# A hybrid retention, gating and convolution layer on one core: a ninth couple in the up product, two weight sums made by adding transfers, and three steps placed elsewhere

## The chip, the cores and the metric

The kernel runs on one core of a Trainium2 chip. The metric is the device time of one execution in microseconds (us); lower is better. A run here is one execution, and the times before are those of three runs.

## The reference

One layer of an encoder over 512 positions of width 1024, in float32:

```python
h = rmsnorm(x, g_pre_mix);  q, k, v, g, u, sv, a_ret, a_sgu = split(h @ w_in)
y_ret = (layernorm(retention(rotary(q), rotary(k), v)) * silu(g)) @ w_ret_o      # both directions, 4 heads
y_sgu = (gelu(u) * (w_spatial @ layernorm(gelu(sv)) + b_spatial)) @ w_sgu_o      # 128-position chunks
x = x + rmsnorm((sigmoid(a_ret) * y_ret + sigmoid(a_sgu) * y_sgu) @ w_out, g_post_mix)
h2 = rmsnorm(x, g_pre_ffn)
hid = depthwise_conv3(h2 @ w_up) + conv_b            # w_up is 1024 x 5632
a, b = split(hid, 2)
y = x + rmsnorm((gelu(a) * b) @ w_down, g_post_ffn)  # w_down is 2816 x 1024
```

## The kernel before, in words

All weights lie in one tensor `wall` of 146 blocks of 128 x 1024 (512 KB). A block or half block is loaded into a `raw` buffer (four of them) by a transfer that SP issues. It is then split into two float32r parts, so that three matmuls give nearly float32 precision: `split` (L112 to L114) has ACT round the value into the high part (L97) and DVE subtract that from the value into the low part (L114). The parts lie in nine `w4` buffers; `w_get` prepares weights up to eight half blocks ahead of their use, and a buffer comes free when PE has used it.

Where a product is big enough, four blocks of it are made by seven products of half size in place of eight (a Strassen-like scheme, `Pair`). `Pair.part1` makes four products, `part2` one, `part3` two, each of 12 matmuls of 256 columns (L915). A plain block (`f_block`) is 24 matmuls of 512 columns (L289 to L291). For a pair, `w_form` loads two blocks (B11, B12, B22, B21) and makes four sums of half blocks: T1 = B12 + B11 (L196), T3 = B12 + B22 in the place of B12 (L197), T2 = T1 + B22 (L199) and T4 = T2 + B21 in the place of T2 (L202). In the up product all four are DVE additions of 128 x 512.

The stages on which the change bears, in order of time:

- **The u blocks** (from 200 to 246 us). Four plain blocks, then pairs. Beside them the layer norm of `sv` is made: `sv_stats` (statistics of one row tile, DVE), `sv_scale` (POOL makes reciprocal roots and shifts from the statistics of all four tiles), `sv_norm(q)` (ACT scales four tiles of half q). These stand where `tc.issue_after(i)` puts them: behind instruction i.
- **The up product** (472 to 672 us). There are 22 tiles i, of two blocks each (a and b). Tiles 4 to 19 are done as eight couples, one after the other: a couple (i, i+1) does the blocks of tile i as a `Pair` and those of tile i+1 as two plain blocks; tiles 20 and 21 are plain. `tile_done` makes the convolution (`conv`, L1226 to L1233), the gate (`gated`), and at given tiles `down_forms`: the sums and splits of activations that the down product needs. Their low parts `fl` are made by an adding transfer that POOL issues (L1252).
- **The down product** (672 to 771 us), in two passes (columns 0 to 511, then 512 to 1023). Each of nine steps j takes weights "q" (768 wide) and their sums "t" (1024 wide, made by DVE at L217, L221 and L222), split into `dh` and `dl`, and does seven products (L1351). Steps of whole tiles stand between (L1367). Beside the steps 2 to 5 of pass two, `first_share` squares pass one's result and multiplies it by gffn (L1421, DVE).

No planner is written in the kernel. The framework orders each engine's instructions when the program is built, within the order of data and the `issue_after` marks; from then on every engine works through its list in order.

Of the kernel before, what the change touches and what calls it, by code (L numbers as in the profile page):

```python
# [13 lines left out]
ALU = mybir.AluOpType  # L14
# [3 lines left out]
S = 512  # L18
NT = S // P
# [8 lines left out]
SV0, U0, GATE0, GATE1 = 24, 32, 40, 72  # L28
# [9 lines left out]
UP0 = DOWN0 - 2 * NF  # L38
EARLY = 4
QK = (4, 0, 5, 1, 6, 2, 7, 3)  # L40
COUPLES = [(i, i + 1) for i in range(4, 20, 2)]

PRE, FFNG, LNG, LNB = 0, 8, 16, 24
CW, CB = 32, 32 + 3 * 2 * NF
# [5 lines left out]
def tile_block(ctx: ExitStack, tc, xT, x, wall, par, cs, wsp, bsp, gpost, gffn, out):  # L50
    nc = tc.nc
# [57 lines left out]
    def as32(t):  # L109
        return t.bitcast(F32)  # L110

    def split(hi, lo, src):  # L112
        copy(hi, src)
        nc.vector.tensor_sub(lo, src, as32(hi))  # L114

# [4 lines left out]
    i = 0  # L122
    while i < NW:
        pair = [(f, i) for f in FORMS]
        if i == SV0:
# [3 lines left out]
            i = U0  # L129
# [3 lines left out]
        elif GATE0 <= i < GATE1:  # L133
            units += pair[:4] + [("blk", i + 2)] + pair[4:] + [("blk", i + 3)]
            i += 4
        elif i == UP0 + 2 * COUPLES[0][0]:
            for a, b in COUPLES:
                pair = [(f, UP0 + 2 * a) for f in FORMS]
                units += pair[:4] + [("blk", UP0 + 2 * b)] + pair[4:] + [("blk", UP0 + 2 * b + 1)]
            i = UP0 + 2 * COUPLES[-1][1] + 2  # L140
        elif i == DOWN0:
# [9 lines left out]
    v = nc.vector  # L151
    w_ready, w_pos, w_held, w_raw = {}, [0, 0], [0], {}
# [32 lines left out]
    def w_form(form, i):  # L185

        if form == "B11":
            a, b = raw_tile(), raw_tile()
            nc.sync.dma_start(a, wall[i])
            nc.sync.dma_start(b, wall[i + 1])  # L190
            w_raw["B11"], w_raw["B12"] = a[:, :S], a[:, S:]
            w_raw["B22"], w_raw["B21"] = b[:, :S], b[:, S:]
        elif form == "T1":
            t = raw_tile()
            w_raw["T1"], w_raw["T2"], w_raw["T3"], w_raw["T4"] = t[:, :S], t[:, S:], w_raw["B12"], t[:, S:]
            nc.vector.tensor_add(w_raw["T1"], w_raw["B11"], w_raw["B12"])  # L196
            nc.vector.tensor_add(w_raw["T3"], w_raw["B12"], w_raw["B22"])  # L197
            eng = nc.vector if i < GATE0 or i >= UP0 else nc.gpsimd
            eng.tensor_tensor(out=w_raw["T2"], in0=w_raw["T1"], in1=w_raw["B22"], op=ALU.add)  # L199
        elif form == "T4":  # L200
            eng = nc.vector if i < GATE0 or i >= UP0 else nc.gpsimd
            eng.tensor_tensor(out=w_raw["T4"], in0=w_raw["T2"], in1=w_raw["B21"], op=ALU.add)  # L202
        w = slot("wf", 0, 1088)
        lo, hi = w[:, AT_64 : AT_64 + S], w[:, S + AT_192 : 2 * S + AT_192]
        split(hi, lo, w_raw[form])
        return hi, lo

    def w_down(form, i):
# [584 lines left out]
    def sv_stats(ts):  # L793
        for t in ts:
            for nh in range(2):
                v.bn_stats(out=sst[:, t, nh, :], in_=svz[t, nh])
            v.bn_aggr(out=smv[:, t, :], in_=sst[:, t].rearrange("p a b -> p (a b)"))
# [3 lines left out]
        rsqrt(srstd, smv[:, :, 1], 1.0, NT)  # L801
        shift(sshift, srstd)

    def sv_norm(q):
        for t in range(NT):
            scaled_to(svz[t, q], srstd[:, t : t + 1], sshift[:, t : t + 1])


# [164 lines left out]
    for j in range(UW):  # L973
        with tc.issue_after(summed) if j == 0 else ExitStack():
            o = f_block(xh, xl, KD)
        u = U_HOMES.pop()()
        i = v.tensor_mul(two(u), in_turn(o), two(rbc)).ins
        g = nc.scalar.activation(out=u, in_=u, func=AF.Gelu_apprx_tanh).ins
        uT.append(u)
        with tc.issue_after(i):  # L980
            sv_stats(((0, 1), (2,), (3,), ())[j])
        if j == 2:
            sv_scale()
    with tc.issue_after(g):
        sv_norm(0)
    for j in range(UW // 2, KD // 2):
        p = Pair(AF.Gelu_apprx_tanh, lambda: U_HOMES.pop()(), None, rbc)
        p.part1()
        if late:
            late.part3()  # L990
        p.part2()
        late = p
        uT += p.t
        if j == UW // 2:
            with tc.issue_after(p.copied):
                sv_norm(1)
    yh, yl = [], []

    def mix(j):
# [288 lines left out]
    def tile_done(i, o):  # L1288
        gated(*(conv(t, 2 * i + s_) for s_, t in enumerate(o)))
        if i < COUPLES[-1][1]:  # L1290
            if i in (7, 9, 11, 13, 17):
                down_forms(len(dforms))
        elif len(dforms) < EAGER:
            down_forms(len(dforms))
# [13 lines left out]

    couples = dict(COUPLES)
    i = 0  # L1310
# [100 lines left out]
    gpf = []  # L1411
    qn = [small("q", 4, 4) for _ in range(NT)]
    zg = []

    def first_share(t):
        zg.append(blk(n="zg"))
        for i in range(2):
            src = c4[2 * (t // 2) + i][:, (t % 2) * 256 : (t % 2 + 1) * 256]
            j = tmp("junk")
            nc.scalar.activation(out=j[:, :256], in_=src, func=AF.Square, scale=D ** -0.5, accum_out=qn[t][:, 2 + i : 3 + i])  # L1420
            v.tensor_mul(zg[t][:, i * 256 : (i + 1) * 256], src, gpf[0][:, i * 256 : (i + 1) * 256])  # L1421
        v.tensor_add(qn[t][:, 0:1], qn[t][:, 2:3], qn[t][:, 3:4])


# [140 lines left out]
def _up(a):  # L1565

    for i, _ in COUPLES:
        b, c = a[2 * i].reshape(P, 2, S), a[2 * i + 1].reshape(P, 2, S)
# [88 lines left out]
```

## Time and profile before

| | |
|---|---|
| three runs, median (lowest to highest) | 786.4 us (786.27 to 786.45) |
| the profiled execution, its own time | 787.56 us |
| its span, first to last instruction | 785.8 us |
| busy: PE, DVE, ACT, POOL | 99%, 80%, 59%, 13% of the span |
| granted TensorE clock | 0.997 |

The profiled execution is 1.16 us slower than the median of the runs, and its own time is 1.76 us longer than its span. In the timeline each matmul stands with its start, and with an end that is modelled: a matmul of 256 columns is shown as 0.28 us long although the next one starts 0.11 us later. So PE counts as busy through a pause that is shorter than this tail, and what PE loses is read from the distance of two starts.

### The profile page before, as it was taken

The page shows a single profiled execution, that of the slowest core. Times are in us where ns is not written, and L with a number is a line of the kernel's source. Part 1 is how long each engine was busy: PE and PEld are TensorE (multiplying, and loading weights), DVE is VectorE, ACT ScalarE, POOL GpSimd, SP SyncE. Part 2 cuts the span into 40 slices and gives each one's busy share as a digit, 9 for nine tenths or more (in the row PEclk, how much of TensorE's full clock was granted, in tenths as well). Part 3 has the DMA queues.
Part 4 walks back from the last instruction along what each step waited for, and adds up shares of the span by engine and source line. Part 5 has one row for each costly group of instructions (what it writes and reads, how often), then busy time and mean ns, then how long its engine had stood idle before and what let it go on. Part 6 is the DMA issues. An engine that isn't in the chain of part 4 may idle for free.

```text
span 785.8 us, 13253 instructions
## 1 busy us (share of the span) xinstructions
PE 777.3 (99%) x5067; PEld 720.5 (92%) x5067; DVE 626.2 (80%) x1067; ACT 467.2 (59%) x848; POOL 104.4 (13%) x132
## 2 busy tenths in 40 slices
PE   9999999999999999999999999999999999999996
PEld 8888998998899999999998898999999998999996
DVE  6467987788777877867765679989999889877887
ACT  6555558689375534444444776657777578744442
POOL 0040001130011111032210210001111012200001
PEclk9999999999999999999999999999999999999998
DMA  8782224463223333223349111435555365633244
GB/s 285 268 260 90 81 81 161 108 133 128 75 82 108 108 108 108 98 92 108 134 166 330 68 68 40 122 108 141 141 148 148 108 195 115 170 114 111 103 163 161
DMA packets 35888, 104.78 MB, mean 133 GB/s; under 512 B 4400, under 2 KB 6320, under 8 KB 35824
## 3 DMA queue, kind: packets, MB, share of 16 engines
q1 hardware_dynamic: 27936, 87.81, 32.6%
q0 software_dynamic: 7024, 14.95, 9.0%
q10 hardware_dynamic: 864, 1.18, 0.4%
q8 instruction: 39, 0.64, 0.3%
q14 instruction: 25, 0.20, 0.1%
HBM read 91.34 MB, written 4.19 MB: 122 GB/s over the span
## 4 chain that ended last, share of the span: by engine, by line
PE 96%; DVE 1%; ACT 1%; issue 1%; POOLq 0%; POOL 0%; DVEq 0%; ACTq 0%
PE ps L915 21%; PE ps L289 13%; PE ps L291 13%; PE ps L290 13%; PE ps L1351 10%; PE ps L744 5%; PE ps L623 4%; PE ps L625 4%; PE ps L624 4%; PE ps L1088 2%; PE ps L1086 2%; PE ps L1087 2%; PE ps L1367 2%; PE ps L1008 1%; PE ps L409 1%
## 5 line engine op out<-in xcount | busy, mean ns | idle before, releaser
L114 DVE TENSOR_TENSOR wl<-raw,wh 128x1024 fp32r<-128x1024 f32 (+1 forms) x88 | 100.6, 1152 | 55.6 <-issue 19.1
L97 ACT ACTIVATE wf<-raw 128x512 fp32r<-128x512 f32 x126 | 75.6, 623 | 85.8 <-PE ps L290 39.8
L97 ACT ACTIVATE wh<-raw 128x1024 fp32r<-128x1024 f32 (+2 forms) x92 | 89.2, 982 | 29.1 <-DMA raw<-wall 16.8
L915 PE MATMUL ps<-sh,wf 128*128 128x256 f32 x576 | 105.8, 276 | 0.5 <-ACT u L97 0.3
L114 DVE TENSOR_TENSOR wf<-raw,wf 128x512 fp32r<-128x512 f32 x126 | 92.3, 745 | 15.2 <-ACT wf L97 14.3
L915 PEld LDWEIGHTS ps<-sh,wf 128*128 128x128 f32 x576 | 91.8, 192 | 1.7 <-ACT u L97 1.1
L289 PE MATMUL ps<-h2h,wh 128*128 128x512 f32 (+1 forms) x256 | 90.6, 354 | 0.0
L290 PE MATMUL ps<-h2l,wh 128*128 128x512 f32 (+1 forms) x256 | 90.4, 353 | 0.0
L291 PE MATMUL ps<-h2h,wl 128*128 128x512 f32 (+1 forms) x256 | 90.4, 353 | 0.0
L915 PE MATMUL ps<-sl,wf 128*128 128x256 f32 x288 | 79.2, 275 | 0.0
L1351 PE MATMUL ps<-dl,fh 128*128 128x256 f32 x216 | 59.7, 276 | 0.3 <-DVE dl L114 0.3
L1351 PE MATMUL ps<-dh,fh 128*128 128x256 f32 x216 | 59.4, 275 | 0.0
L1351 PE MATMUL ps<-dh,fl 128*128 128x256 f32 x216 | 59.4, 275 | 0.0
L915 PEld LDWEIGHTS ps<-sl,wf 128*128 128x128 f32 x288 | 55.2, 192 | 0.4
L97 ACT ACTIVATE dh<-raw 128x768 fp32r<-128x768 f32 (+1 forms) x36 | 33.7, 951 | 35.7 <-DVE raw L222 21.8
L291 PEld LDWEIGHTS ps<-h2h,wl 128*128 128x128 f32 x256 | 48.6, 190 | 5.1
L289 PEld LDWEIGHTS ps<-h2h,wh 128*128 128x128 f32 x256 | 48.6, 190 | 4.5
L290 PEld LDWEIGHTS ps<-h2l,wh 128*128 128x128 f32 x256 | 48.6, 190 | 4.5
L625 PE MATMUL ps<-wh,xl 128*128 128x512 f32 x128 | 48.5, 379 | 0.0
L624 PE MATMUL ps<-wl,xh 128*128 128x512 f32 x128 | 48.5, 379 | 0.0
L623 PE MATMUL ps<-wh,xh 128*128 128x512 f32 x128 | 48.5, 380 | 0.0
L915 PE MATMUL ps<-xh,wf 128*128 128x256 f32 x240 | 44.0, 276 | 0.0
(343 smaller groups left out, 2187.3 us busy)
## 6 DMA issues: line engine op xcount, KB each, us to landing
raw<-wall SPq DMA_DIRECT2D x144, 512.0 KB, 3.6
x<-x SPq DMA_DIRECT2D x24, 256.0 KB, 5.6
fl<-gp POOLq DMA_DIRECT2D x12, 256.0 KB, 4.0
swap<-qkraw POOLq DMA_DIRECT2D x16, 128.0 KB, 4.3
x<-x POOLq DMA_DIRECT2D x8, 256.0 KB, 2.3
fl<-fs POOLq DMA_DIRECT2D x8, 256.0 KB, 3.3
xT<-xT SPq DMA_DIRECT2D x7, 256.0 KB, 5.3
xT<-xT POOLq DMA_DIRECT2D x4, 256.0 KB, 4.0
```

Source lines behind the costliest of these rows:

```text
L97: return nc.scalar.activation(out=o, in_=i, func=AF.Copy)
L114: nc.vector.tensor_sub(lo, src, as32(hi))
L289: nc.tensor.matmul(o, ah, bh, start=start, stop=False, skip_group_check=skip)
L290: nc.tensor.matmul(o, ah, bl, start=False, stop=False, skip_group_check=skip)
L291: nc.tensor.matmul(o, al, bh, start=False, stop=stop, skip_group_check=skip)
L623: nc.tensor.matmul(acc[t], xh[k][:, c], turns(wh[:, f]), start=k == 0, stop=False)
L624: nc.tensor.matmul(acc[t], xh[k][:, c], turns(wl[:, f]), start=False, stop=False)
L625: part_end[0] = nc.tensor.matmul(acc[t], xl[k][:, c], turns(wh[:, f]), start=False, stop=k == KD - 1)
L744: nc.tensor.matmul(bank[t], a_[:, c], turns(w_[:, f]), start=first and k == i == 0, stop=last and k == 3 and i == 2, skip_group_check=True,)
L915: self.last = nc.tensor.matmul(o, w_[:, c], a_, start=first and k == n == 0, stop=k == 3 and n == 2, skip_group_check=True,)
L1086: nc.tensor.matmul(o, ah, turns(bh), start=k == 0, stop=False)
L1351: nc.tensor.matmul(o, a_[:, c], turns(w_[:, f]), start=j == t == i == 0, stop=j == DP - 1 and i == 2 and n not in (M2, M3, M4), skip_group ...
```

## The change

- `COUPLES` gets a ninth couple, tiles 20 and 21. The tiles behind which `down_forms` is called become 7, 9, 11, 13, 17, 19, 20 and (by the other branch) 21; before, they were 7, 9, 11, 13, 17, 19, 20, 21 as well, but 20 and 21 are now finished together.
- In the up product T3 and T4 are no longer DVE additions. POOL issues a transfer that reads B22, or B21, again from `wall` in HBM and adds it to the half block in place (256 KB each). T3's is issued behind T1's addition, T4's behind the split of T2.
- The statistics of `sv`: tiles 0 and 1 behind the first u block as before, 2 and 3 both behind the second. `sv_scale` follows the second u block, not the third. `sv_norm(0)` stands behind the third block's gelu, two tiles of `sv_norm(1)` behind the fourth's, and the other two behind the copy in the first pair, where all four stood before.
- In pass two the multiplications by gffn are issued behind the last split's subtraction that has been written so far (`low[0]`).

```diff
-COUPLES = [(i, i + 1) for i in range(4, 20, 2)]
+COUPLES = [(i, i + 1) for i in range(4, 22, 2)]
...
+    low = [None]
+
     def split(hi, lo, src):
         copy(hi, src)
-        nc.vector.tensor_sub(lo, src, as32(hi))
+        low[0] = nc.vector.tensor_sub(lo, src, as32(hi)).ins
...
             nc.vector.tensor_add(w_raw["T1"], w_raw["B11"], w_raw["B12"])
-            nc.vector.tensor_add(w_raw["T3"], w_raw["B12"], w_raw["B22"])
+            if i < UP0:
+                nc.vector.tensor_add(w_raw["T3"], w_raw["B12"], w_raw["B22"])
+            else:
+                nc.gpsimd.dma_start(w_raw["T3"], wall[i + 1, :, :S], accum_op=ALU.add)
             eng = nc.vector if i < GATE0 or i >= UP0 else nc.gpsimd
             eng.tensor_tensor(out=w_raw["T2"], in0=w_raw["T1"], in1=w_raw["B22"], op=ALU.add)
-        elif form == "T4":
-            eng = nc.vector if i < GATE0 or i >= UP0 else nc.gpsimd
+        elif form == "T4" and i < UP0:
+            eng = nc.vector if i < GATE0 else nc.gpsimd
             eng.tensor_tensor(out=w_raw["T4"], in0=w_raw["T2"], in1=w_raw["B21"], op=ALU.add)
...
         split(hi, lo, w_raw[form])
+        if form == "T2" and i >= UP0:
+            nc.gpsimd.dma_start(w_raw["T4"], wall[i + 1, :, S:], accum_op=ALU.add)
         return hi, lo
...
-    def sv_norm(q):
-        for t in range(NT):
+    def sv_norm(q, ts=range(NT)):
+        for t in ts:
             scaled_to(svz[t, q], srstd[:, t : t + 1], sshift[:, t : t + 1])
...
         with tc.issue_after(i):
-            sv_stats(((0, 1), (2,), (3,), ())[j])
-        if j == 2:
+            sv_stats(((0, 1), (2, 3), (), ())[j])
+        if j == 1:
             sv_scale()
-    with tc.issue_after(g):
-        sv_norm(0)
+        if j > 1:
+            with tc.issue_after(g):
+                sv_norm(j - 2, range((NT, 2)[j - 2]))
...
             with tc.issue_after(p.copied):
-                sv_norm(1)
+                sv_norm(1, range(2, NT))
...
-            if i in (7, 9, 11, 13, 17):
+            if i in (7, 9, 11, 13, 17, 19, 20):
                 down_forms(len(dforms))
...
-            v.tensor_mul(zg[t][:, i * 256 : (i + 1) * 256], src, gpf[0][:, i * 256 : (i + 1) * 256])
+            with tc.issue_after(low[0]):
+                v.tensor_mul(zg[t][:, i * 256 : (i + 1) * 256], src, gpf[0][:, i * 256 : (i + 1) * 256])
```

What the change moves on the engines, at three places. In these rows a name carries the number of its buffer, which differs between the two programs; code lines behind the edit are 2 to 9 higher in the changed kernel.

ACT, about the fourth u block (its gelu is `u_2370` before, `u_2374` now) and the first pair (its first copy out of PSUM is `u_2377` before, `u_2379` now). Before:

```order
L97 ACTIVATE wf_2342<-raw_2338 128x512
L97 ACTIVATE wf_2382<-raw_2339 128x512
L978 ACTIVATE u_2370<-u_2370 128x512
L715 ACTIVATE sv_1802<-sv_1802,sshift,srstd 128x512
L715 ACTIVATE sv_1803<-sv_1803,sshift,srstd 128x512
L715 ACTIVATE sv_2197<-sv_2197,sshift,srstd 128x512
L715 ACTIVATE sv_2199<-sv_2199,sshift,srstd 128x512
L97 ACTIVATE u_2377<-ps_2379 128x256
```

The same place now:

```order
L722 ACTIVATE sv_1802<-sv_1802,sshift,srstd 128x512
L722 ACTIVATE sv_1803<-sv_1803,sshift,srstd 128x512
L722 ACTIVATE sv_2197<-sv_2197,sshift,srstd 128x512
L722 ACTIVATE sv_2199<-sv_2199,sshift,srstd 128x512
L97 ACTIVATE wf_2346<-raw_2342 128x512
L97 ACTIVATE wf_2384<-raw_2343 128x512
L985 ACTIVATE u_2374<-u_2374 128x512
L722 ACTIVATE sv_1978<-sv_1978,sshift,srstd 128x512
L722 ACTIVATE sv_1979<-sv_1979,sshift,srstd 128x512
L97 ACTIVATE u_2379<-ps_2381 128x256
```

Two scalings stand between the gelu and the pair's first copy where there were four, and the first four stand ahead of the block's weights.

POOL, in the middle of the up product (the weights of couples (14, 15) and (16, 17)): `fl` are the low parts of `down_forms`, `raw` the half blocks T3 and T4. Before:

```order
L1252 DMA fl_6268<-fs_6262 128x512
L1252 DMA fl_6273<-gp_5569 128x512
L1252 DMA fl_6278<-gp_5558 128x512
L1252 DMA fl_6501<-fs_6495 128x512
L1252 DMA fl_6506<-gp_5779 128x512
L1252 DMA fl_6511<-gp_5768 128x512
```

The same place now:

```order
L1260 DMA fl_6268<-fs_6262 128x512
L1260 DMA fl_6273<-gp_5569 128x512
L202 DMA raw_6334<-wall 128x512
L1260 DMA fl_6278<-gp_5558 128x512
L212 DMA raw_6357<-wall 128x512
L1260 DMA fl_6501<-fs_6495 128x512
L1260 DMA fl_6506<-gp_5779 128x512
L202 DMA raw_6567<-wall 128x512
```

T3's transfer stands behind two `fl` transfers of the same couple, and T4's behind three and T3's.

DVE, in pass two of the down product: `dl` are low parts of weights, `raw` the sums t, `zg` the multiplications by gffn. Before:

```order
L114 TENSOR_TENSOR dl_8085<-raw_8082,dh_8084 128x768
L217 TENSOR_TENSOR raw_8120<-raw_8082 128x512
L1421 TENSOR_TENSOR zg_8240<-c_7379,gpf_8116 128x256
L221 TENSOR_TENSOR raw_8120<-raw_8120,raw_8082 128x256
L1421 TENSOR_TENSOR zg_8240<-c_7380,gpf_8116 128x256
L222 TENSOR_TENSOR raw_8120<-raw_8120,raw_8082 128x256
L1422 TENSOR_TENSOR q_8045<-q_8045 128x1
L1421 TENSOR_TENSOR zg_8304<-c_7379,gpf_8116 128x256
L1421 TENSOR_TENSOR zg_8304<-c_7380,gpf_8116 128x256
```

The same place now:

```order
L116 TENSOR_TENSOR dl_8149<-raw_8146,dh_8148 128x768
L224 TENSOR_TENSOR raw_8184<-raw_8146 128x512
L1431 TENSOR_TENSOR q_8109<-q_8109 128x1
L1431 TENSOR_TENSOR q_8110<-q_8110 128x1
L228 TENSOR_TENSOR raw_8184<-raw_8184,raw_8146 128x256
L1431 TENSOR_TENSOR q_8111<-q_8111 128x1
L1431 TENSOR_TENSOR q_8112<-q_8112 128x1
L229 TENSOR_TENSOR raw_8184<-raw_8184,raw_8146 128x256
L116 TENSOR_TENSOR dl_8189<-raw_8184,dh_8188 128x1024
```

The multiplications have left this place; they stand in four lots of two between the splits of later steps.

## The prediction

> **What bounds the kernel now.** I read the page first, then the chain that ended last, then PE's timeline wherever the chain leaves PE.
>
> ```profile
> PE 777.3 (99%) x5067; PEld 720.5 (92%) x5067; DVE 626.2 (80%) x1067; ACT 467.2 (59%) x848; POOL 104.4 (13%) x132
> ```
>
> PE is busy for 99% of the span. So an edit pays only if it takes matmuls away, or ends a pause between two matmuls. The chain (start, length, what) gives the price of a couple and of two plain tiles:
>
> ```profile
> 492.98 5.36 PE ps L915 x48
> ...
> 513.20 5.36 PE ps L915 x48
> ...
> 611.90 5.36 PE ps L915 x48
> ...
> 631.64 5.36 PE ps L915 x48
> ...
> 672.10 18.76 PE ps L1351 x168
> ```
>
> Each L915 row of 48 matmuls opens a couple, and the L1351 row opens the down product. A couple takes 631.64 - 611.90 = 19.74 us. The last one so ends at 651.38, and the two plain tiles behind it take 672.10 - 651.38 = 20.72. The first couple took 513.20 - 492.98 = 20.22, hence 0.48 over its price. A matmul of 256 columns is 5.36 / 48 = 0.112 us; one of 512 is 20.72 / 96 = 0.216.
>
> The other pauses stand in PE's timeline (start, shown length, what). First the pairs of u:
>
> ```profile
> 224.71 0.28 PE L915 MATMUL ps<-xh,wf 128*128 128x256 f32 x1
> 225.31 0.38 PE L915 MATMUL ps<-sh,wf 128*128 128x256 f32 x1 [0.33 <-ACT u L97]
> 225.53 0.28 PE L915 MATMUL ps<-sl,wf 128*128 128x256 f32 x1
> ...
> 226.98 0.39 PE L915 MATMUL ps<-xh,wf 128*128 128x256 f32 x2
> 227.39 0.38 PE L915 MATMUL ps<-sh,wf 128*128 128x256 f32 x1
> ...
> 232.52 0.28 PE L915 MATMUL ps<-xl,wf 128*128 128x256 f32 x1
> 232.92 0.38 PE L915 MATMUL ps<-sh,wf 128*128 128x256 f32 x1
> ```
>
> The starts should be 0.112 apart. They are 0.60 (0.49 lost), 0.41 for two (0.19) and 0.40 (0.29) apart, and the first matmul after each pause takes 0.22 (0.11 lost, three times): 1.3 us in all. Who held PE stands in the timelines of ACT, DVE and POOL:
>
> ```profile
> 220.50 1.15 ACT L97 ACTIVATE wf<-raw 128x512 fp32r<-128x512 f32 x2 [3.51 <-issue]
> ...
> 222.08 2.91 ACT L715 ACTIVATE sv<-sv,sshift,srstd 128x512 f32<-128x512 f32 x4
> 224.90 0.36 ACT L97 ACTIVATE u<-ps 128x256 f32<-128x256 f32 x1
> ```
> ```profile
> 216.69 1.28 DVE L796 BATCH_NORM_STATS2 sst<-sv 128x6 f32<-128x512 f32 x2
> ```
> ```profile
> 218.78 0.51 POOL L448 TENSOR_SCALAR rs<-smv 128x4 f32<-128x4 f32 x1 [42.93 <-DVE smv L797]
> ...
> 220.95 0.20 POOL L712 TENSOR_TENSOR sshift<-sshift,srstd 128x4 f32<-128x4 f32 x1
> ```
>
> PE waits for the copy u at 224.90, which stands behind four scalings of sv (2.91 us). Those were ready only after POOL's 221.15, while ACT had idled 3.51 us before 220.50.
>
> Then pass two of the down product:
>
> ```profile
> 740.95 0.28 PE L1351 MATMUL ps<-dh,fh 128*128 128x256 f32 x1
> 741.49 0.38 PE L1351 MATMUL ps<-dl,fh 128*128 128x256 f32 x1 [0.27 <-DVE dl L114]
> ...
> 755.67 0.28 PE L1351 MATMUL ps<-dh,fh 128*128 128x256 f32 x1
> 755.93 0.38 PE L1351 MATMUL ps<-dl,fh 128*128 128x256 f32 x1
> ```
> ```profile
> 737.61 0.42 DVE L1421 TENSOR_TENSOR zg<-c,gpf 128x256 f32<-128x256 f32 x1
> ...
> 740.21 2.09 DVE L114 TENSOR_TENSOR dl<-raw,dh 128x1024 fp32r<-128x1024 f32 x2 [1.11 <-ACT dh L97]
> ```
> ```profile
> 739.12 1.79 ACT L97 ACTIVATE dh<-raw 128x1024 fp32r<-128x1024 f32 x2 [3.70 <-PE ps L1351]
> ```
>
> Pauses of 0.43 and 0.15, each with its slow restart of 0.10: 0.78 us. The multiplications zg stand between DVE's sums of t; ACT can round t only at 739.12, and DVE's low part comes 0.5 us late.
>
> **The ninth couple.** It takes the place of two plain tiles: 20.72 - 19.74 = 0.98 us less PE, certain as long as PE is fed. The Trainium skill (TensorE: Matmul & The Clock Gate, "Back-to-back issue gap") gives N / 2.4 + 2.5 ns; for 512 columns that is the trace's 0.216, for 256 it is 0.109 against 0.112, and by it the term would be 1.2. The row decides.
>
> **sv.** The fourth tile's statistics stand one u block earlier (24 x 0.216 = 5.2 us), and POOL's 2.4 us (218.78 to 221.15) follow them. DVE has two blocks' other work there, so I take 4 us of the 5.2: scales at about 217.2, four scalings to 220.1, in ACT's idle time. Two more follow the gelu (222.08 to 223.5), so the copy comes at 223.5 and not 224.90, before PE needs it at 224.82. If the scales were 1 us later, wf would slip into PE's lead and nothing more. Of 1.29 us I take 1.15 as gone, with 0 and 1.29 as ends.
>
> **Pass two.** Without two zg of 0.33 (0.42 long, overlapping) around each t, the chain of sums, ACT and dl is 0.7 us or more ahead at 740; the pauses were 0.43 and 0.15. Later the eight zg stand between dl's that are then early. I take 0.75 of 0.78, with 0 as the other end.
>
> **T3 and T4.** These windows show busy times of PE, PEld, DVE, ACT, POOL:
>
> ```profile
> 492.90:513.10 20.20, 20.20 (x134) 18.42 (x133) 19.44 (x31) 13.77 (x25) 1.83 (x2) 1.00 0.49 145
> ...
> 592.10:611.80 19.70, 19.70 (x134) 18.41 (x133) 18.45 (x32) 14.68 (x28) 2.57 (x3) 1.00 0.56 148
> ```
>
> DVE is at 19.44 of 20.2 us in the first couple, where PE loses 0.48. Two additions fewer (about 0.6 each, spacing below) leave it some air; I take 0.4 of the 0.48. In later couples PE loses nothing now, so DVE's 1.2 us a couple buys nothing there. What the transfers cost is bounded by these rows (issues of 256 KB with us to landing, then POOL and ACT):
>
> ```profile
> fl<-gp POOLq DMA_DIRECT2D x12, 256.0 KB, 4.0
> ...
> sb<-wall POOLq DMA_DIRECT2D x4, 256.0 KB, 5.7
> ```
> ```profile
> 583.94 0.87 POOL L1252 DMA_DIRECT2D fl<-gp  x1 [0.33 <-ACT fl L1251]
> ```
> ```profile
> 589.61 0.63 ACT L97 ACTIVATE wf<-raw 128x512 fp32r<-128x512 f32 x1
> ```
>
> T3's transfer is queued behind this fl, so it starts at 584.8 and lands at 588.8 to 590.5; ACT wants it at 589.61. The wait is 0 to 0.9 us, T4's is like it. Behind it on ACT stand the convolution's rounds and copies out of PSUM, then DVE; both have more idle time per couple than that (ACT 19.7 - 14.68, DVE 19.7 - 18.45 + 1.2). PE: 0.
>
> **What the couple costs: the way into the down product.** DVE must do the ninth couple's seven split halves, T1, T2 and three subtractions where it had four block splits, beside the gates of tiles 20 and 21 and three `down_forms`.
>
> ```profile
> 648.80:687.70 38.90, 38.90 (x250) 36.00 (x250) 36.07 (x61) 30.33 (x49) 8.85 (x11) 1.00 0.60 142
> ```
> ```profile
> 686.49 1.23 DVE L114 TENSOR_TENSOR dl<-raw,dh 128x1024 fp32r<-128x1024 f32 x1
> 687.63 0.69 DVE L217 TENSOR_TENSOR raw<-raw 128x512 f32<-128x512 f32 x1
> 688.23 1.22 DVE L114 TENSOR_TENSOR wl<-raw,wh 128x1024 fp32r<-128x1024 f32 x1
> 689.37 0.42 DVE L221 TENSOR_TENSOR raw<-raw,raw 128x256 f32<-128x256 f32 x1
> 689.70 0.42 DVE L1270 TENSOR_TENSOR gp<-gp 128x256 f32<-128x256 f32 x1
> ```
> ```profile
> 688.13 0.28 PE L1351 MATMUL ps<-dl,fh 128*128 128x256 f32 x1
> ```
> ```profile
> L1233 DVE SCALAR_TENSOR_TENSOR cv<-ps,part,cv 128x511 f32<-128x511 f32 x28 | 20.7, 743 | 0.1
> ```
>
> DVE has 2.8 us idle in these 38.9, and its tightest low part is ready at 687.72 for a use at 688.13: 0.41 us ahead. By the starts, DVE's steps take 1.14 (1024 wide), 0.60 (512), 0.33 (256), and 0.66 for L1233 (0.743 long against 0.69). The added work is 9 x 0.60 + 2 x 1.14 + 3 x 0.33 - 4 x 1.14 = 4.1 us, less 1.2 for T3 and T4 of the eighth couple. Is there room? I walked the changed order from the ninth couple's last subtraction (it follows products that end 12 x 0.216 = 2.6 us before the down product starts) to the low part of the third t: 8 convolution passes, 3 of 512, 9 of 256, 2 of 1024, 1 of 768 (0.87) are 13.2 us. Starting 0.3 after its product, that ends 10.9 us after the down product's start. PE uses the third t there after two steps of 42 matmuls and 19 more, 103 x 0.112 = 11.5 us. So 0.6 us are left if nothing on DVE waits for ACT. I expect a few short waits and take 0.3 us of PE; the ends are 0 and 2.2, where the old idle stays (2.8 - 0.6).
>
> **The sum.** 0.98 + 1.15 + 0.75 + 0.4 - 0.3 = 3.0 us. The profiled execution's 787.56 would become 784.6 (span 782.8); the median of the runs, 1.16 lower, goes from 786.4 to **783.4**. A measurement of this kernel tells about 0.2% (1.6 us) from no change; below 784.8 is faster.
>
> **Rivals.**
>
> - *DVE stays full into the down product.* The walk assumed no waits; if DVE idles as before, PE loses 2.2 us at the third and fourth t, and 3.3 - 2.2 = 1.1 us of gain is left: 785.3, no change. For it: 0.41 us of lead even now. Against: the deferred `fl` splits let dl go first. 0.19.
> - *The transfers come late; slower.* ACT and DVE take their lists in order, so a late T3 or T4 holds them. DVE has 19.7 - 18.45 + 1.2 = 2.45 us spare a couple; once the two waits together exceed this, each couple grows. At 1.7 us each, 3.4 - 2.45 = 0.95 for nine couples is 8.6 us; less 3.3 gained it is 5.3 slower, 791.7. The result is slower by over 0.2% from 1.5 us a transfer, landing 6.3 us after issue. Against: 4.0 and 5.7 us in the rows. The Trainium skill (SBUF — State Buffer, "SBUF: two separate sides") warns that POOL cannot write a transfer's descriptors while DVE runs an instruction in a two-port mode; that would be this mechanism. The trace bears it out little: with DVE 94% busy over a couple, the issue at 583.94 took 0.87 us. 0.12.
> - *The sv scalings do not leave the way.* If the scales are ready only at 219, or the copy still queues, the 1.3 us stay: 784.5, still faster. 0.11.
> - The forecast itself: 0.58.
>
> **How the numbers follow.** Faster are the forecast and the third rival, 0.69. No change is the first, 0.19. Slower is the second, 0.12. The range: below, every term at its best end and no cost, 0.98 + 1.29 + 0.78 + 0.48 = 3.5, and a little for a pause not listed, 782.6. Above, it takes in the first rival with 0.9 us more (PE's restarts, a second late t), 786.2. Left out is the second rival and the far tail of the first, under 2 in 10.
>
> **What would show it.** Right: 9 couples 19.74 us apart, first one included; the sv pauses gone, with four L722 scalings ending before ACT's 220.5; no pause at 740; adding transfers landing within 6 us. Wrong: starts of couples over 19.9 apart with ACT's wf waiting for `raw<-wall` on POOL's queue (second rival); PE waiting for dl between 4 and 18 us into the down product (first).

## The result, and the profile after

| | before | after |
|---|---|---|
| median of six runs (lowest to highest) | 786.42 us (786.27 to 787.64) | 790.68 us (789.82 to 793.21) |
| ratio, 95% interval | | 1.0053, 1.0037 to 1.0070 |
| the profiled execution: time, span | 787.56, 785.8 us | 791.38, 789.6 us |

The changed kernel is 4.3 us slower, where the prediction had 3.0 us faster, with slower at a chance of 0.12. The busy times and the chain that ended last, from the page after:

```profile
PE 776.7 (98%) x5103; PEld 721.8 (91%) x5103; DVE 622.4 (79%) x1061; ACT 470.4 (60%) x857; POOL 119.7 (15%) x150
PE 91%; ACT 3%; DMA 2%; DVE 2%; issue 1%; POOL 0%; POOLq 0%; DVEq 0%; ACTq 0%
```

DVE has 3.8 us less work than before and ACT 3.2 more, both small against their idle time, so a sum of busy times would blame neither. The chain tells more: 9% of it lies outside PE, most of that on ACT, DVE and transfers.

**What was to go is gone.** ACT's timeline after (start, length, what), and PE's at the only pause that is left among the pairs of u:

```profile
216.90 2.91 ACT L722 ACTIVATE sv<-sv,sshift,srstd 128x512 f32<-128x512 f32 x4
220.34 1.15 ACT L97 ACTIVATE wf<-raw 128x512 fp32r<-128x512 f32 x2 [0.53 <-PE ps L297]
...
221.92 1.51 ACT L722 ACTIVATE sv<-sv,sshift,srstd 128x512 f32<-128x512 f32 x2
223.33 0.36 ACT L97 ACTIVATE u<-ps 128x256 f32<-128x256 f32 x1
```
```profile
225.93 0.39 PE L922 MATMUL ps<-xh,wf 128*128 128x256 f32 x2
226.35 0.38 PE L922 MATMUL ps<-sh,wf 128*128 128x256 f32 x1
```

The four scalings stand at 216.90 (expected: 217.2), the copy u comes at 223.33 (expected: 223.5), and of 1.28 us 0.29 are left. The first couple takes 19.80 us, so of its 0.48 us 0.06 are left, and pass two's 0.78 do not occur any more. PE's timeline has three new pauses:

```profile
613.97 0.28 PE L922 MATMUL ps<-sh,wf 128*128 128x256 f32 x1
615.49 0.38 PE L922 MATMUL ps<-sh,wf 128*128 128x256 f32 x1 [1.24 <-ACT c L97]
...
665.30 0.38 PE L298 MATMUL ps<-h2h,wl 128*128 128x512 f32 x1
666.80 0.38 PE L922 MATMUL ps<-h2h,wf 128*128 128x256 f32 x1 [1.12 <-ACT c L97]
...
676.20 0.28 PE L1359 MATMUL ps<-dh,fa 128*128 128x256 f32 x1
679.42 0.55 PE L1359 MATMUL ps<-dh,fh 128*128 128x256 f32 x1 [2.95 <-DVE cv L1241]
679.76 0.42 PE L1359 MATMUL ps<-dl,fh 128*128 128x256 f32 x1
...
682.11 0.37 PE L1359 MATMUL ps<-dl,fh 128*128 128x256 f32 x1
682.31 0.27 PE L1359 MATMUL ps<-dh,fl 128*128 128x256 f32 x1
```

By the starts, 615.49 - 613.97 less 0.11 is 1.4 us, and 0.1 for the slow matmul behind it: 1.5. At 665.30 it is 1.28 and 0.1: 1.4. At 676.20 it is 3.1, and then the matmuls start 0.21 apart and not 0.11 until 682.31, which is another 1.5: 4.6 us. That makes 7.5 us new; 2.2 of pauses and 0.98 of matmuls are gone, and small differences elsewhere give back 0.5: 3.8 us, which is the spans' difference.

The first pause stands in the timelines of POOL and ACT:

```profile
605.08 0.86 POOL L212 DMA_DIRECT2D raw<-wall  x1
```
```profile
610.52 0.64 ACT L1248 ACTIVATE cv<-cv 128x512 f32<-128x512 f32 x1
613.35 0.63 ACT L97 ACTIVATE wf<-raw 128x512 fp32r<-128x512 f32 x1 [2.18 <-DMA raw<-wall]
613.88 0.76 ACT L1234 ACTIVATE cv<-ps,part 128x512 f32<-128x512 f32 x1
614.55 0.61 ACT L97 ACTIVATE wf<-raw 128x512 fp32r<-128x512 f32 x1
615.07 0.37 ACT L97 ACTIVATE c<-ps 128x256 f32<-128x256 f32 x1
```

T4's transfer, issued at 605.08, is waited for until 613.35, some 8.2 us. ACT idles 2.18 us, and the copy c out of PSUM that PE needs stands three instructions behind. This is the second rival's mechanism at one place. The windows (busy PE, PEld, DVE, ACT, POOL, clock, share of the DMA engines, GB/s) show what was on the DMA engines:

```profile
595.00:600.00 5.00, 5.00 (x28) 4.47 (x27) 5.00 (x11) 2.12 (x5) 0.00 (x0) 1.00 0.12 48
...
606.00:608.00 2.00, 2.00 (x18) 1.95 (x17) 1.61 (x2) 1.21 (x2) 0.00 (x0) 1.00 1.02 180
608.00:610.00 2.00, 2.00 (x11) 1.76 (x10) 1.62 (x4) 1.59 (x3) 0.00 (x0) 1.00 1.09 193
```

From 606 to 610 the DMA engines are full: POOL issued three `fl` transfers, T3 and T4 within 4 us (601.09 to 605.08), and SP's blocks of `wall` stand beside them. That this made T4 late is argued from these rows. One couple earlier the engines are as full (1.11 from 586 to 588), and there T4, issued at 585.07, made ACT wait only 0.16 us, until 591.15. So a full stretch does not by itself cost PE anything.

The other two pauses have their own chain, in order of time (start, length, what), and ACT's timeline beside it:

```profile
657.88 4.69 DMA fl<-gp
...
663.64 4.45 DMA fl<-fs
```
```profile
662.66 0.63 ACT L1259 ACTIVATE fl<-fh 128x512 fp32r<-128x512 f32 x1 [0.80 <-DMA fl<-gp]
663.87 0.63 ACT L97 ACTIVATE fh<-gp 128x512 fp32r<-128x512 f32 x1 [0.58 <-DMA fl<-gp]
...
666.39 0.36 ACT L97 ACTIVATE c<-ps 128x256 f32<-128x256 f32 x1
668.17 0.63 ACT L1259 ACTIVATE fl<-fh 128x512 fp32r<-128x512 f32 x1 [1.42 <-DMA fl<-fs]
```

ACT waits 2.8 us for adding transfers of `down_forms`, not for T3 or T4: 1.4 us of it ahead of the copy c, which starts at 666.39 where PE stands from 665.5 on, and all of it ahead of the convolution. At 676.3 PE wants the bank of PSUM (where the `ps` tiles lie) that block a of tile 21 still fills, for the second product of the down product; DVE's last pass over it starts only at 678.53:

```profile
678.53 0.74 DVE L1241 SCALAR_TENSOR_TENSOR cv<-ps,part,cv 128x511 f32<-128x511 f32 x1
```

### The profile page after: what moved, and what is told of

It reads as the page before. It is cut to its first block, busy times and chain, and to the rows that moved or that the text cites. A ratio compares the mean times of both kernels' runs of the same rounds, so it can differ in the third digit from the quotient of the medians.

```text
span 789.6 us, 13390 instructions
## 1 busy us (share of the span) xinstructions
PE 776.7 (98%) x5103; PEld 721.8 (91%) x5103; DVE 622.4 (79%) x1061; ACT 470.4 (60%) x857; POOL 119.7 (15%) x150
## 4 chain that ended last, share of the span: by engine, by line
PE 91%; ACT 3%; DMA 2%; DVE 2%; issue 1%; POOL 0%; POOLq 0%; DVEq 0%; ACTq 0%
PE ps L922 20%; PE ps L296 12%; PE ps L298 12%; PE ps L297 12%; PE ps L1359 10%; PE ps L751 5%; PE ps L630 4%; PE ps L632 3%; PE ps L631 3%; PE ps L1096 2%; PE ps L1094 2%; PE ps L1095 2%; PE ps L1375 2%; DMA raw<-wall 1%; PE ps L1016 1%
## 5 line engine op out<-in xcount | busy, mean ns | idle before, releaser
L97 ACT ACTIVATE wf<-raw 128x512 fp32r<-128x512 f32 x133 | 80.1, 623 | 90.8 <-PE ps L297 33.1
L116 DVE TENSOR_TENSOR wf<-raw,wf 128x512 fp32r<-128x512 f32 x133 | 97.9, 750 | 19.3 <-ACT wf L97 19.1
L922 PE MATMUL ps<-sh,wf 128*128 128x256 f32 x608 | 111.4, 275 | 1.3 <-ACT c L97 1.2
L922 PEld LDWEIGHTS ps<-sh,wf 128*128 128x128 f32 x608 | 96.9, 192 | 2.1 <-ACT c L97 1.4
L296 PE MATMUL ps<-h2h,wh 128*128 128x512 f32 (+1 forms) x240 | 84.5, 352 | 0.0
L297 PE MATMUL ps<-h2l,wh 128*128 128x512 f32 (+1 forms) x240 | 84.3, 351 | 0.0
L298 PE MATMUL ps<-h2h,wl 128*128 128x512 f32 (+1 forms) x240 | 84.3, 351 | 0.0
L922 PE MATMUL ps<-sl,wf 128*128 128x256 f32 x304 | 83.6, 275 | 0.0
L922 PEld LDWEIGHTS ps<-sl,wf 128*128 128x128 f32 x304 | 58.3, 192 | 0.5
L116 DVE TENSOR_TENSOR dl<-raw,dh 128x768 fp32r<-128x768 f32 (+1 forms) x36 | 39.1, 1087 | 9.7 <-ACT dh L97 5.5
```

Of the source, the lines that this page charges most:

```text
L97: return nc.scalar.activation(out=o, in_=i, func=AF.Copy)
L116: low[0] = nc.vector.tensor_sub(lo, src, as32(hi)).ins
L296: nc.tensor.matmul(o, ah, bh, start=start, stop=False, skip_group_check=skip)
L297: nc.tensor.matmul(o, ah, bl, start=False, stop=False, skip_group_check=skip)
L298: nc.tensor.matmul(o, al, bh, start=False, stop=stop, skip_group_check=skip)
L922: self.last = nc.tensor.matmul(o, w_[:, c], a_, start=first and k == n == 0, stop=k == 3 and n == 2, skip_group_check=True,)
```

## Experiments

Each kernel was timed in turns with the kernel before (786.6 to 786.9 us in these comparisons); the ratio has a 95% interval. The theories are A (the transfers of T3 and T4 are the cause), B (the ninth couple is), and within B: C (ACT is held by transfers of `fl`), D (DVE has too much work there), E (a PSUM bank).

### Which part of the change

**e1**, the changed kernel with T3 and T4 on DVE:

```diff
-            if i < UP0:
-                nc.vector.tensor_add(w_raw["T3"], w_raw["B12"], w_raw["B22"])
-            else:
-                nc.gpsimd.dma_start(w_raw["T3"], wall[i + 1, :, :S], accum_op=ALU.add)
+            nc.vector.tensor_add(w_raw["T3"], w_raw["B12"], w_raw["B22"])
...
-        elif form == "T4" and i < UP0:
-            eng = nc.vector if i < GATE0 else nc.gpsimd
+        elif form == "T4":
+            eng = nc.vector if i < GATE0 or i >= UP0 else nc.gpsimd
...
-        if form == "T2" and i >= UP0:
-            nc.gpsimd.dma_start(w_raw["T4"], wall[i + 1, :, S:], accum_op=ALU.add)
```

> The changed kernel with T3 and T4 made by DVE again; ninth couple, sv and zg as changed. In the changed kernel PE lost 1.5 us at 614 us (ACT waits for T4's transfer, 8.2 us after its issue) and 6.0 us around the start of the down product (1.4 at 665; 3.1 and a slow restart of 1.5 at 676). Theory A, the adding transfers are the cause of all of it, since they delay the last couple too: all 7.5 us go, 783 to 784 us. Theory B, the ninth couple is the cause at the end of the up product, the transfers only of the pause at 614: that pause goes, the 6.0 us stay, 789 to 790 us, slower than before; DVE having 1.2 us more work in the last couple, the pauses may even be longer.

**e2**, the changed kernel with eight couples:

```diff
-COUPLES = [(i, i + 1) for i in range(4, 22, 2)]
+COUPLES = [(i, i + 1) for i in range(4, 20, 2)]
...
-            if i in (7, 9, 11, 13, 17, 19, 20):
+            if i in (7, 9, 11, 13, 17):
```

> The changed kernel with eight couples; transfers, sv and zg as changed. Theory A (transfers): late transfers stay, and what they delay at the end, 788 to 789 us. Theory B (ninth couple): the pauses at 665 and 676 are gone and the start of the down product is as before; gained are sv 1.0, pass two 0.8 and the first couple 0.5, against that stands now and then a late transfer of up to 1.5 us: 784 to 786 us.

**e3**, both of these edits together: what remains is the sv and the zg part.

> The kernel before with only the sv and the zg parts. Both theories: pauses at 225 to 233 us go but for 0.3, pauses at 741 and 755 go, the first couple's 0.5 stays: 786.4 - 1.0 - 0.8 = 784.6 us. If it is 786 or more, these two parts do not carry their gain to the end.

**e4**, the kernel before with the ninth couple alone (e2's edit the other way).

> The kernel before with only the ninth couple. Theory A (transfers are the cause): 0.98 us of matmuls less and at most 0.3 lost, 785.4 to 785.8 us. Theory B (ninth couple): 0.98 us less and about 6 lost at the start of the down product, 790.5 to 792 us, with PE waiting there for a copy on ACT and for a convolution pass on DVE.

Measured: e1 788.78 us, ratio 1.0038 (1.0025 to 1.0050); e2 785.92, 0.9990 (0.9981 to 0.9998); e3 785.19, 0.9987 (0.9976 to 0.9998); e4 791.16, 1.0055 (1.0043 to 1.0068). All four fall where B put them, or within 0.6 us of it. The couple alone costs 4.4 us; with the transfers gone e1 still has both late pauses, and no pause at 614. The part of the transfers of T3 and T4 is smaller: e1 is 1.9 us faster than the changed kernel. PE's timeline of e1:

```profile
665.31 0.38 PE L917 MATMUL ps<-h2h,wf 128*128 128x256 f32 x1 [1.14 <-ACT c L97]
...
677.95 0.48 PE L1354 MATMUL ps<-dh,fh 128*128 128x256 f32 x1 [2.98 <-DVE cv L1236]
```

This profiled execution took 790.86 us, 2.1 more than e1's median, so the 6.2 us that its two pauses cost with their slow matmuls (1.4 and 4.8) are more than the median lost. By the medians the couple's end costs about 788.78 - (785.19 - 0.98) = 4.6 us.

e2's profile shows a pause of 0.6 us at 614, which e3 lacks, and e3's shows 0.2 us in the first couple, which e2 lacks. The medians of the two are 0.7 us apart, but their intervals overlap; h1 below prices the transfers better.

### Why the ninth couple loses

ACT's timeline where the last sets of `down_forms` begin and where it waits for `fl` transfers, first in e1, then in e3:

```profile
653.55 0.64 ACT L97 ACTIVATE fh<-fs 128x512 fp32r<-128x512 f32 x1
...
659.93 0.63 ACT L97 ACTIVATE fh<-fs 128x512 fp32r<-128x512 f32 x1 [1.54 <-DMA fl<-fs]
661.15 0.63 ACT L1254 ACTIVATE fl<-fh 128x512 fp32r<-128x512 f32 x1 [0.59 <-DMA fl<-gp]
662.37 0.63 ACT L97 ACTIVATE fh<-gp 128x512 fp32r<-128x512 f32 x1 [0.59 <-DMA fl<-gp]
...
664.89 0.36 ACT L97 ACTIVATE c<-ps 128x256 f32<-128x256 f32 x1
666.71 0.63 ACT L1254 ACTIVATE fl<-fh 128x512 fp32r<-128x512 f32 x1 [1.45 <-DMA fl<-fs]
```
```profile
638.24 0.63 ACT L97 ACTIVATE fh<-fs 128x512 fp32r<-128x512 f32 x1 [1.96 <-DVE fs L1272]
645.97 0.63 ACT L97 ACTIVATE fh<-fs 128x512 fp32r<-128x512 f32 x1 [1.75 <-DVE fs L1272]
...
665.28 0.42 ACT L97 ACTIVATE fa<-gp 128x256 fp32r<-128x256 f32 x1 [0.20 <-DMA fl<-fs]
```

Each `fh<-fs` opens a set. With plain tiles at the end the sets behind tiles 17 and 19 start at 638 and 646; with the ninth couple the framework puts them at 653.6 and 659.9, right behind one another, and ACT waits 4.2 us in place of 0.2. The instructions that wait do not read what the transfers make. They wait for memory: in the program built from e1's kernel each of the four writes its result to the place of a tile that is the source of the very transfer it waits for, and that place is free only when the transfer has read it. The three at 659.93, 661.15 and 662.37 take the places of the `fs` and the two `gp` of the set behind tile 17, and the one at 666.71 that of the `fs` of the set behind tile 19. So the copy c at 664.89, for which PE stands, is held by the transfers of the set behind tile 17 alone.

**f1**: the last three sets make `fl` on DVE.

```diff
-        apart = split_added if j < EAGER else split
+        apart = split_added if j < 5 else split
```

> The kernel of e1 (ninth couple, no adding transfers for T3 and T4) whose last three sets of down_forms make their low parts fl by DVE's subtraction, without ACT's negated copy and POOL's adding transfer. e1 took 788.8 us and lost 1.4 us at 664 and 4.8 us at 675. Theory C (ACT, in order, stands waiting for the fl transfers, 2.8 us between 660 and 669, and that makes the copy and the convolution late): the pause at 664 goes and that at 675 shrinks below 2, 784 to 786 us. Theory D (too much work for ACT and DVE together at the end of the ninth couple, wherever it stands): ACT has 4.8 us less, DVE 5.4 us more, the pauses change place but not their sum, 788 to 790 us.

795.27 us, ratio 1.0103 (1.0088 to 1.0117). A miss for both: the time grew by 6.5 us, more than the 5.4 us that DVE got. The windows from 648 to 690 (columns as above) of e3, e1 and f1:

```profile
648.00:690.00 42.00, 42.00 (x283) 39.26 (x283) 39.24 (x67) 32.09 (x51) 8.48 (x11) 1.00 0.60 145
```
```profile
648.00:690.00 42.00, 37.89 (x270) 35.88 (x270) 37.56 (x65) 33.70 (x57) 10.30 (x12) 0.96 0.68 158
```
```profile
648.00:690.00 42.00, 35.86 (x251) 33.10 (x250) 40.22 (x71) 28.81 (x49) 3.13 (x4) 0.98 0.33 94
```

In e1 DVE is less busy than in e3 although it is behind: it waits for ACT. In f1 it is nearly full (40.22 of 42 us), and PE waits for it and for roundings on ACT that stand behind DVE's sums. But f1 is no clean test of C: the set behind tile 17 keeps its transfers, and ACT still waits 3.4 us for them at the same place, DVE 1.5.

**f2**: the sets behind other tiles.

```diff
-            if i in (7, 9, 11, 13, 17, 19, 20):
+            if i in (7, 9, 11, 13, 15, 17, 19):
```

> The kernel of e1 with down_forms called behind tiles 7, 9, 11, 13, 15, 17, 19 and 21 in place of 7, 9, 11, 13, 17, 19, 20 and 21: one set less (3.5 us of ACT, 1.7 us of DVE) at the end of the ninth couple. Theory D: both pauses lose what ACT is relieved of, 664 goes and 675 falls from 4.8 to about 1, 783.5 to 785 us. Theory C: the waits for the fl transfers of the sets that remain stay, so that half of the 6.2 us stays, 785.5 to 787 us.

**f3**: one set made in the down product.

```diff
-            if i in (7, 9, 11, 13, 17, 19, 20):
+            if i in (7, 9, 11, 13, 17, 19):
...
-    late = list(range(EAGER, DP))
+    late = list(range(len(dforms), DP))
...
-        if j == 4:
+        if j in (3, 4):
             down_forms(late.pop(0))
```

> The kernel of e1 with the last set of down_forms that is made in the up product moved into the down product (step 3 of pass one). Theory D: ACT and DVE are relieved at the end of the ninth couple, but this last set stood behind tile 21, after PE's pauses began: the pause at 664 stays, that at 675 shrinks by less than 2 us, 787 to 788.5 us. Theory C: as D, since the transfers ACT waits for belong to the sets before; if the set comes late for its step, up to 1 us more.

**f4**: tile 21's first convolution earlier.

```diff
             o = [f_block(h2h, h2l, KD)]
+            ca = conv(o[0], 2 * (i + 1)) if i == 20 else None
             p.part2()
...
-            tile_done(i + 1, o)
+            tile_done(i + 1, o, ca)
...
-    def tile_done(i, o):
-        gated(*(conv(t, 2 * i + s_) for s_, t in enumerate(o)))
+    def tile_done(i, o, ca=None):
+        gated(*(ca if ca and not s_ else conv(t, 2 * i + s_) for s_, t in enumerate(o)))
```

> The kernel of e1, but block a of tile 21 has its convolution written before the couple's second part, so that its three passes leave the end and its PSUM bank is free early. In e1 the second product of the down product waits for just that bank. If the bank is what counts (theory E): the pause at 675 falls from 4.8 to under 1.5, 785 to 786 us, with 664 as it is. If the amount of work at the end counts (D): the pause moves to the next bank, that of block b, and keeps more than half of its length, 787 to 788.5 us; the pause at 664 grows by up to 0.8 us, since one more pass stands ahead of ACT's copy.

f2 took 790.25 us (1.0028 to 1.0052), f3 789.94 (1.0025 to 1.0049), f4 789.42 (1.0021 to 1.0039): none is better than e1, and all three miss both of their ranges: f2 by 3.3 us or more, f3 by 0.4, f4 by 0.9. In f2 the waits for `fl` are nearly gone (0.5 us), but the framework laid out another order, the last three sets come up to 3.5 us later, and PE waits 1.2 us for a copy at 661 and 1.1 and 0.55 for `dl` at 684 and 687. So a loss is there without C's waits too. In f4 the pause at 675 is gone as theory E said, but at 664 PE now loses 3.7 us, where e1 lost 1.3:

```profile
663.69 0.38 PE L293 MATMUL ps<-h2h,wl 128*128 128x512 f32 x1
667.60 0.38 PE L917 MATMUL ps<-h2h,wf 128*128 128x256 f32 x1 [3.53 <-ACT c L97]
```

So the bank is only where the delay shows. Moving work in these three ways does not help.

**g1**: the last three sets without adding transfers; **k1**: the set behind tile 17 too (4 in place of 5).

```diff
+    def no_add(hi, lo, src):
+        copy(hi, src)
+        nc.scalar.activation(out=lo, in_=as32(hi), func=AF.Copy, scale=-1.0)
...
-        apart = split_added if j < EAGER else split
+        apart = no_add if 5 <= j < EAGER else split_added if j < EAGER else split
```

> The kernel of e1, but the last three sets of down_forms leave out the adding transfers of fl (fl stays the negated high part; the same work on ACT and DVE, nine transfers of POOL fewer, so their buffers come free at once). Theory C (ACT held by the fl transfers: it waits 4.2 us for them between 659 and 668 in e1, 0.2 us in e3): the waits go, and with them the pause at 664 and most of the one at 675, 784 to 786 us. Theory D (the amount of work on DVE at the end): the pauses keep their sum, 788 to 789 us.

> As g1, but the set of down_forms behind tile 17 leaves out its adding transfers too (four sets, 12 transfers). In g1 the pause at 664 stayed (1.7 us), and ACT still waited 2.5 us just ahead of it for transfers, those of this set. Theory C: these waits go and the pause at 664 with them; the pause at 675 stays at about 1.8 as in g1; 786.0 to 786.8 us. Theory D: the pause at 664 stays or its time moves into the one at 675, 788 us as g1.

**g2**: no third tap in tiles 20 and 21; **k2**: k1 and g2 together.

```diff
-        v.scalar_tensor_tensor(
-            out=c[:, 0 : S - 1], in0=o[:, 1:S], scalar=col(CW + 3 * m + 2), in1=c[:, 0 : S - 1],
-            op0=ALU.mult, op1=ALU.add,
-        )
+        if m < 40:
+            v.scalar_tensor_tensor(
+                out=c[:, 0 : S - 1], in0=o[:, 1:S], scalar=col(CW + 3 * m + 2), in1=c[:, 0 : S - 1],
+                op0=ALU.mult, op1=ALU.add,
+            )
```

> The kernel of e1, but the convolution of tiles 20 and 21 leaves out its third tap (4 passes of DVE, 0.66 us each, 2.6 us). Theory D (DVE's work at the end of the ninth couple goes one to one into PE's pauses, as the 5.4 us added in f1 cost 6.5): the time falls by 2.6 or more, since a shorter pause also spares the slow restart of 1.5 us, 784.7 to 786.2 us. Theory C: DVE waits for ACT there, and the passes only fill its waits, 788 to 789 us.

> k1 and g2 together: no adding transfers of fl in four sets, no third tap in tiles 20 and 21 (2.6 us of DVE). If waiting for transfers (C) and the amount of work on DVE (D) each hold a part of the loss: no pause over 0.3 us at 660 to 680, 784.2 to 785 us, and the ninth couple then pays. If something else bounds the end (ACT's own work), 786 us or more.

**k3**: four sets without `fl` (`two_parts` returns `h_, h_`).

> As k1, but these four sets make no fl at all (the products take fh in its place): besides the transfers, 12 negated copies leave ACT (0.52 us each, 6.2 us) and 12 buffers are not used. If ACT's work is a bound of its own beside C: clearly under k1, 784 to 785 us, with no pause at 664 and under 0.5 at 675. If DVE's work is (D): within 0.5 us of k1, and the pause at 675 stays over 1 us.

Measured: g1 788.12 us (1.0001 to 1.0023), g2 788.74 (1.0012 to 1.0035), k1 785.63 (0.9975 to 0.9993), k2 784.89 (0.9967 to 0.9985), k3 786.18 (0.9985 to 1.0003). g1 and g2 each landed where the other theory put them: g1 2.1 us above C's range and inside D's, g2 2.5 us above D's and inside C's. Each alone shortened the pause at 675 (to 1.8 and 1.6 us), kept the one at 664, and gained 0.7 us and nothing; in g2 PE waited later in their place (0.6 at 703, 1.0 at 729 to 731). k1 then took the waits of the set behind tile 17 away, and the pause at 664 went with them. ACT's list is nearly the same in k1 as in e1; the copy c even stands one instruction later. In ACT's timeline of k1 the set that began at 659.93 in e1 begins at 658.46, and the copy c comes at 663.25, before PE's 664.01; in e1 it came at 664.89:

```profile
658.46 0.63 ACT L97 ACTIVATE fh<-fs 128x512 fp32r<-128x512 f32 x1
...
663.25 0.36 ACT L97 ACTIVATE c<-ps 128x256 f32<-128x256 f32 x1
```
```profile
664.01 0.27 PE L917 MATMUL ps<-h2h,wf 128*128 128x256 f32 x1
...
674.87 0.35 PE L1358 MATMUL ps<-dh,fh 128*128 128x256 f32 x1 [1.41 <-ACT fa L97]
```

k1 is 3.2 us faster than e1. The pause of 1.6 us that it has left falls to 0.6 with the four passes of DVE out of the way, and k2 is 0.7 us faster still, in its range, though not without a pause over 0.3 us:

```profile
673.62 0.38 PE L1359 MATMUL ps<-dh,fh 128*128 128x256 f32 x1 [0.40 <-DVE cv L1232]
```

k3 takes 6.2 us of ACT's work away and is not faster than k1; its pause at 675 is still 1.4 us. So of the 4.6 us by which the couple's end is slow in e1, 3.2 are C, ACT waiting in order for the transfers, and 0.7 are D, DVE's work, which shows only once C is gone; ACT's own work is no bound, and the last 0.7 stay open. These kernels leave work out, so they tell the cause and are no versions. The transfers' load on the DMA engines went with them. It can have acted only through how late `fl` lands: e1's profile shows no engine waiting for a transfer of weights between 640 and 690 us.

### Versions

**h1**, e3 with T3 and T4 by transfer in the first couple alone (`i != UP0 + 8` and `i == UP0 + 8` in place of `i < UP0` and `i >= UP0`):

> The kernel of e3 (sv and zg parts alone) with T3 and T4 made by adding transfers in the first couple only, where DVE is at 19.4 of 20.2 us and PE loses 0.5. If the transfers relieve DVE there, the pause at 507 goes as it did in the changed kernel, 784.7 against 785.2 us of e3. If POOL's transfers cost something on their own, 785.2 or more.

> h1 once more, beside m1 and m2: 784.8 us. It is the faster version unless the ninth couple now keeps over half of its 0.98 us.

**h2**, e3 with the ninth couple in front:

```diff
-COUPLES = [(i, i + 1) for i in range(4, 20, 2)]
+COUPLES = [(i, i + 1) for i in range(2, 20, 2)]
```

> The kernel of e3 with a ninth couple too, but in front (tiles 2 and 3), so that tiles 20 and 21 stay plain in front of the down product. Theories C and D both put the loss at the place where the last couple meets the down product's weights and the last down_forms: the end stays as in e3 without a pause, and the 0.98 us of the couple is gained, 784.2 us. If any couple without plain tiles behind it overfills DVE (it is already full in the first couple, 0.5 us of pause there), the pause comes at 475 to 510 us, and the time is 785.5 to 788 us.

**m1**, h1 with the ninth couple, transfers there too, and `fl` of four sets on POOL; **m2** without the transfers in the ninth couple:

```diff
+    def on_pool(hi, lo, src):
+        copy(hi, src)
+        nc.gpsimd.tensor_tensor(out=lo, in0=src, in1=as32(hi), op=ALU.subtract)
...
+        apart = on_pool if 4 <= j < EAGER else split_added if j < EAGER else split
```

> A complete kernel made from what k1 and k2 showed: ninth couple, sv and zg parts; T3 and T4 by adding transfers in the first and the ninth couple only; the last four sets of down_forms have fl subtracted by POOL (1.3 to 1.85 us each by POOL's rows of this shape), in place of ACT's negated copy and an adding transfer that lands 4 to 5 us later. Theory C and D together: buffers come free 3 us earlier and DVE has 1.2 us less in the ninth couple; pauses at 660 to 680 under 1 us in sum, 784.0 to 785.0 us, about the 784.8 of h1. If POOL's subtractions queue up (12 x 1.6 = 19 us within some 28) or slow DVE beside them, the waits return: 786 to 788 us.

> As m1, but T3 and T4 of the ninth couple on DVE (1.2 us more DVE there). Theory D: 0.5 to 1.2 us slower than m1. If the late landing of T4 counts for more than DVE's 1.2 us: not slower than m1.

h1 took 784.83 and, again, 784.65 us: ratios 0.9969 (0.9957 to 0.9980) and 0.9970 (0.9958 to 0.9981). It beats both kernels, and e2, whose interval lies above: the transfers in the seven other couples cost about 1.1 us (785.92 - 784.83), of which e2's trace shows the 0.6 at 614. Its two adding transfers land in 3.9 and 4.0 us, with no `fl` beside them, and the first couple loses nothing. h2 took 790.35 us (1.0029 to 1.0065), a miss: PE loses it at the front, where DVE is still making the sums and splits of h2 (`sl`) and the weights come late:

```profile
483.42 0.48 PE L291 MATMUL ps<-h2h,wh 128*128 128x512 f32 x1 [1.69 <-ACT wh L97]
```

m1 and m2 took 795.75 and 795.92 us (1.0092 to 1.0126 and 1.0098 to 1.0127), 11 us over what was hoped for m1 and 8 over its second case, in which POOL's subtractions slow DVE; that this case came, and at what price, stands in the last section. m2 is not slower than m1, so D's 0.5 to 1.2 us did not show. No placement or means tried here lets a ninth couple pay.

## Why the prediction was wrong

- **The ninth couple's 0.98 us**: right as matmuls. Six couples stand 19.74 apart and the first 19.80; the seventh takes 21.24 and the ninth 21.13 with their pauses.
- **sv, 1.15 us**: right, 0.99 measured. **Pass two, 0.75**: right, 0.78. **First couple, 0.4**: right in size, 0.42 in the trace. Not all of it is the transfers' doing: without them e3's first couple takes 19.96, with them h1's takes 19.74, and the medians of the two are 0.4 apart, with intervals that overlap. The third rival, that the scalings stay in the way, did not occur.
- **T3 and T4, zero**: wrong in size. The bound of 4.0 and 5.7 us to landing came from transfers that stand apart; in couples with `fl` transfers beside them they took up to 8.2. The second rival's point of decision, 6.3 us, was passed, but PE lost time by it in one couple only: 1.5 us in the profiled execution, about 1.1 by e2 and h1. That rival expected a loss in every couple and 791.7 us; that the time came out near this is luck, since most of it has another cause.
- **The way into the down product, 0.3 us with ends 0 and 2.2**: this is the step that failed; it cost 6.0 us. It walked DVE's list from the ninth couple's last subtraction "if nothing on DVE waits for ACT", and looked at the weights `dl` 10 us into the down product. Where it went wrong is earlier and on the other engine: ACT's list, in which the sets of `down_forms` behind tiles 17 and 19 had moved 12 to 15 us later, right ahead of those behind 20 and 21. ACT waited 2.8 us in it for transfers (4.2 in e1), with PE's copies behind. The first rival named DVE and a late `dl`, and its sign did not come: PE waited for a copy on ACT and for a bank of PSUM. Its 2.2 us let DVE keep its old idle time and left out new waits of ACT.
- The restart of 1.5 us behind the long pause was in no term of the sum: all pauses of before were short and cost 0.1. Only the range's upper end had 0.9 us for restarts and a second late t together.

## What to carry to other kernels

When a change brings work together at the end of a stage, walk every in-order engine there, and for each instruction ask not only whether its inputs are ready but also who holds the buffer that it writes. A transfer that is free as long as it lands unobserved holds its source and its target: here T3 and T4 took 3.9 and 4.0 us where nothing stood beside them (h1), and up to 8.2 where `fl` transfers did. Any buffer that the transfer reads can be the one that the next set is waiting to write. A busy time that falls is no comfort: DVE had 3.8 us less to do over the whole, and PE waited for it, because DVE itself had waited for ACT.

## What the runs showed of the hardware

**A long pause costs more than itself.** After 1.0 to 1.75 us of idle time PE restarts with a few slow matmuls at most. After 2.52 us in e4 there was one at most; after 2.95 us in the changed kernel and 2.98 in e1 13 and 16 matmuls were at half rate, 0.213 us in place of 0.112; after 4.3 in m1, 21. A slow matmul costs 0.10, so the 13 are most of the 1.5 us. The granted clock says the same: in the changed kernel it is 1.00 from 676 to 678 us, 0.50 from 680 to 682 and 1.00 again from 684. In f4, 3.53 us were followed by one slow matmul only. The Trainium skill (TensorE: Matmul & The Clock Gate, "Part 1: The HAM clock gate") has PE fall to half its clock after an idle window of about 3.4 us that runs freely, and stay there for about as long. The half rate agrees, and roughly the length of the slow stretch: 2.9 us in the changed kernel, 3.5 in e1, 4.6 in m1. In the length of the pause the runs differ from it: here 2.95 us of idle time were enough, and in f4 3.53 were not.

**POOL's arithmetic stops DVE.** DVE's timeline of m1, beside POOL's subtractions and without them, and POOL's:

```profile
657.60 1.49 DVE L1280 TENSOR_TENSOR fs<-gp,gp 128x256 f32<-128x256 f32 x1
...
660.15 0.41 DVE L1281 TENSOR_TENSOR fs<-fs,gp 128x256 f32<-128x256 f32 x1
...
661.69 1.76 DVE L224 TENSOR_TENSOR raw<-raw 128x512 f32<-128x512 f32 x1
```
```profile
655.67 3.14 POOL L1264 TENSOR_TENSOR fl<-gp,fh 128x512 fp32r<-128x512 f32 x2
661.31 1.59 POOL L1264 TENSOR_TENSOR fl<-fs,fh 128x512 fp32r<-128x512 f32 x1 [2.50 <-ACT fh L97]
```

At 657.60, while POOL works until 658.81, a subtraction of 256 columns takes 1.49 us; at 660.15, with POOL idle, one takes 0.41. The one of 512 at 661.69 ends 0.55 us after POOL's, and alone it takes 0.67 (at 668.59): it hardly ran before POOL had ended. That these stops make up m1's loss is argued from such rows, not shown by a run of its own. The Trainium skill (SBUF — State Buffer, "SBUF: two separate sides") says that a DVE instruction with two inputs in SBUF and a GpSimd instruction that reads SBUF need the same port pair, which the first to start holds for its whole instruction; the trace agrees. The page's other warning, that DVE in a two-port mode keeps POOL from writing a transfer's descriptors, is not needed for the late T4: DVE was idle from 605.06 to 606.39, all through the issue of T4 (605.08 to 605.94), and the DMA engines were full.
